# Average pooling of a 3-D volume: the early store goes back into one queue, and TensorE takes over the wait for the stores

## The chip, the core and the metric

The kernel runs on one core of a Trainium2 chip. The metric is the device time of one execution in microseconds; the kernel before has a median of 91.88 us over three executions (91.84 to 92.04). A core has five engines that run their own instruction streams: TensorE (PE), VectorE (DVE), ScalarE (ACT), GpSimd (POOL) and SyncE (SP). They meet at semaphores, which are small counters. Transfers between the chip's memory (HBM) and the core's on-chip memory (SBUF, 128 partitions) are issued by SP or ACT, each into a queue of its own, and are carried out by 16 DMA engines. A transfer adds 1 to its semaphore 16 times, once for each DMA engine, as the parts land.

## The reference

The input is x, 8 x 32 x 32 x 32 x 32 in float32 (33.55 MB). The output is the mean of each 2 x 2 x 2 window over the last three dimensions, 8 x 32 x 16 x 16 x 16 (4.19 MB):

```python
for i in range(out_d):
    for j in range(out_h):
        for k in range(out_w):
            window = x[:, :, 2*i:2*i+2, 2*j:2*j+2, 2*k:2*k+2]
            result[:, :, i, j, k] = np.mean(window, axis=(-3, -2, -1))
```

## The kernel before

Batch and channel together are 256 rows, which are two halves of 128 partitions (t = 0 and 1). A row of the input is 32768 floats, cut into 128 pieces of KF = 256 floats. The list `plan` cuts each half into four units of 32 pieces, 32 KB per partition and 4 MB in all. The last two units are each loaded and pooled in two parts of 16 pieces, so there are ten loads: six of 4 MB and four of 2 MB. The tile `tin` has five buffers, so the sixth, seventh and eighth unit wait until VectorE is done with the first, second and third.

For each part `pool_unit` runs three VectorE operations: pairs of planes are added (L58), then neighbours in a row (L62), and then pairs of lines, scaled by 1/8, into `obuf` (L65). A small instruction that reads VectorE's accumulator into `dummy` follows each. There is one `obuf` per half, 16 KB per partition.

All ten loads are issued by SP (L77), in order. The first was moved ahead of the opening barrier. Four stores (L92) take the output out. ACT issues the first: 2 KB per partition of half 0, as soon as the first unit is pooled. SP issues the others after all its loads: the remaining 14 KB per partition of half 0, then 14 KB of half 1, which waits for all but the last part, and then the last 2 KB of half 1. A queue's transfers are started in the order of their issue, so the large stores stand behind the loads in SP's queue.

The end of the program is written out by hand (L119 to L161). The list `kept` holds the semaphores that the stores update. The block `closing` has SP's waits for all other semaphores, a barrier of the five engines (L102 in the profile; GpSimd gathers and releases it with semaphores 96 and 97), GpSimd's clearing of the semaphores that are not kept (L151, an instruction for each stretch of numbers), and then, on SP, one EventSemaphore for each kept semaphore (L155): it waits until the store has landed and subtracts what was added, so that the semaphore is back at zero. Nothing stands behind these in the program. In the built program the kept semaphores are 102, 103, 104 and 105: 102 belongs to ACT's store and afterwards to the last load, 103 to 105 each to an early load and then to a store.

Of the kernel before, what the change touches and what calls it, by code (L numbers as in the profile page):

```python
# [1 line left out]

# [4 lines left out]

F32 = mybir.dt.float32
KF = 256


@with_exitstack
def pool_rows(
    ctx: ExitStack,
    tc: tile.TileContext,
    x: bass.AP,
    kernel_size: int,
    out: bass.AP,
):
    nc = tc.nc  # L20
    assert kernel_size == 2, "only kernel_size == 2 supported"

    B, C, D, H, W = x.shape
    P = nc.NUM_PARTITIONS
    assert (B * C, D, H, W) == (2 * P, 32, 32, 32)
    add = mybir.AluOpType.add

    xv = x.rearrange("b c d h w -> (b c) (d h w)")  # L30
    ov = out.rearrange("b c d h w -> (b c) (d h w)")

    pool_in = ctx.enter_context(tc.tile_pool(name="pin", bufs=5))
    pool_out = ctx.enter_context(tc.tile_pool(name="pout", bufs=1))
    obuf = [pool_out.tile([P, 16 * KF], F32, name=f"obuf{t}") for t in range(2)]
    dummy = pool_out.tile([P, 1], F32, name="dummy")


    plan = [
        (0, 0, (32,)),
        (0, 32, (32,)),
        (0, 64, (32,)),
        (0, 96, (32,)),
        (1, 0, (32,)),
        (1, 32, (32,)),
        (1, 64, (16, 16)),
        (1, 96, (16, 16)),  # L50
    ]

    def pool_unit(buf, t, k0, kb):

        od = kb // 8
        a = buf.rearrange("p (o dd e) -> p o dd e", o=od, dd=2)
        b = buf[:, :od * 1024]
        nc.vector.tensor_add(  # L58
            out=b.rearrange("p (o e) -> p o e", o=od), in0=a[:, :, 0], in1=a[:, :, 1])
        bv = b.rearrange("p (e ww) -> p e ww", ww=2)  # L60
        c = buf[:, od * 1024:od * 1536]
        nc.vector.tensor_add(out=c, in0=bv[:, :, 0], in1=bv[:, :, 1])  # L62
        cv = c.rearrange("p (j hh k) -> p j hh k", hh=2, k=16)
        o0 = k0 * KF // 8
        nc.vector.tensor_tensor_reduce(  # L65
            out=obuf[t][:, o0:o0 + od * 256].rearrange("p (j k) -> p j k", k=16),
            in0=cv[:, :, 0], in1=cv[:, :, 1],
            scale=0.125, scalar=0.0, op0=add, op1=add, accum_out=dummy[:, :],
        )

    for t, k0, parts in plan:
        tin = pool_in.tile([P, 32 * KF], F32, tag="tin", name="tin")
        views = []
        o = 0
        for kb in parts:
            v = tin[:, o * KF:(o + kb) * KF]
            nc.sync.dma_start(  # L77
                out=v, in_=xv[t * P:(t + 1) * P, (k0 + o) * KF:(k0 + o + kb) * KF])
            views.append((v, k0 + o, kb))
            o += kb  # L80
        for v, k, kb in views:
            pool_unit(v, t, k, kb)

    for queue, t, k0, kb in [
        (nc.scalar, 0, 0, 2),
        (nc.sync, 0, 2, 14),
        (nc.sync, 1, 0, 14),
        (nc.sync, 1, 14, 2),  # L90
    ]:
        queue.dma_start(  # L92
            out=ov[t * P:(t + 1) * P, k0 * KF:(k0 + kb) * KF],
            in_=obuf[t][:, k0 * KF:(k0 + kb) * KF],
        )


def kernel(tc: tile.TileContext, x: bass.AP, kernel_size: int, out: bass.AP):
    nc = tc.nc
    pool_rows(tc, x, kernel_size, out)  # L100
    tc.close()
    tc.compile()  # L102
    blocks = nc.main_func.blocks

    opening, program = blocks[0].instructions, blocks[tc.starting_block_idx].instructions
    load = next(i for i in program if isinstance(i, mybir.InstDMACopy))
    assert load.engine == nc.sync.engine
    barrier = next(  # L110
        n for n, i in enumerate(opening)
        if i.engine == load.engine and isinstance(i, mybir.InstDrain))
    program.remove(load)
    opening.insert(barrier, load)

    closing = blocks[-1].instructions  # L119
    stores = [  # L120
        i for i in program
        if isinstance(i, mybir.InstDMACopy) and "out_" in i.outs[0].memref]
    kept = [u.id for i in stores for u in i.sync_info.on_update]
    kept = [n for j, n in enumerate(kept) if n not in kept[j + 1:]]
    final = next(
        i for i in closing
        if i.engine == nc.sync.engine and isinstance(i, mybir.InstDrain))
    waits = {w.id: w for w in final.sync_info.on_wait}
    closing[closing.index(final)] = mybir.InstDrain(
        name=final.name, engine=final.engine, ins=[], outs=[], is_reset_sema=False,  # L130
        sync_info=mybir.SyncInfo(
            on_wait=[w for n, w in waits.items() if n not in kept], on_update=[]))


    reset = next(
        n for n, i in enumerate(closing)
        if isinstance(i, mybir.InstDrain) and i.is_reset_sema)
    first, stop = closing[reset].reset_range_start, closing[reset].reset_range_stop
    assert isinstance(closing[reset + 1], mybir.InstISA)
    while len(closing) > reset:  # L140
        closing.pop()
    n = first
    while n < stop:
        m = n
        while m < stop and m not in kept:
            m += 1
        if m > n:
            closing.append(mybir.InstDrain(
                name=nc.get_next_instruction_name(), engine=nc.gpsimd.engine, ins=[], outs=[],
                is_reset_sema=True, reset_range_start=n, reset_range_stop=m))  # L150
            nc.gpsimd.sem_clear(range(n, m))  # L151
        n = m + 1
    for n in kept:
        w = waits[n]
        closing.append(mybir.InstEventSemaphore(  # L155
            name=nc.get_next_instruction_name(), engine=nc.sync.engine, ins=[], outs=[],
            sync_info=mybir.SyncInfo(
                on_wait=[w],
                on_update=[mybir.SyncUpdate(
                    sync_type="semaphore", id=n, ant_name=w.ant_name,  # L160
                    update_mode="sem-sub-imm", update_value=w.wait_value)])))  # L161


# [1 line left out]
_INS = ['x', 'kernel_size']  # L165
_OUTS = [((8, 32, 16, 16, 16), 'float32')]

_NUMBERS = {'kernel_size': 2}


# [26 lines left out]
```

## Time and profile before

| what | value |
|---|---|
| median of three executions | 91.88 us (91.84 to 92.04) |
| profiled execution, its own time | 91.84 us |
| its span, first to last instruction | 86.9 us |
| the time outside the span | 4.94 us |
| VectorE busy | 64.0 us |
| DMA, mean rate over the span | 422 GB/s |
| read, written | 33.55 MB, 4.19 MB |

The span ends with GpSimd's clearing of semaphores. The four EventSemaphores on SP that wait for the stores carry no source line and are not among the instructions of the profile, nor is what the runtime does after the program. The trace does record each update of each semaphore with its time, after the span too; times of updates below are counted from the start of the span, as all others are. "Landing" is the last of a transfer's 16 updates. A row of the instruction list such as "SPq" or "PEldq" is an instruction of that engine's sequencer, not of the engine's arithmetic.

### The profile page before, as it was taken

The numbers are of one execution on the slowest core, as the hardware profiler recorded it, in microseconds if no ns is written. First come the engines' busy times: TensorE is split into PE (matmuls) and PEld (weight loads), VectorE is DVE, ScalarE is ACT, GpSimd is POOL, SyncE is SP. The second block draws the span as 40 slices with busy tenths as digits, with TensorE's granted clock in tenths as the row PEclk, the third lists the DMA queues.
The fourth block names the chain that finished last, engine by engine and source line by source line (L and its number), as shares of the span: only waits on it lengthen the run. The fifth ranks groups of instructions, "written<-read, shape, count | busy, mean of one in ns | idle before, by whom it ended". The sixth has DMA issues, their size and how long they took to land.

```text
span 86.9 us, 90 instructions
## 1 busy us (share of the span) xinstructions
DVE 64.0 (74%) x40; POOL 0.2 (0%) x4
## 2 busy tenths in 40 slices
DVE  0000049992999729994799929994899999999994
POOL 0000000000000000000000000000000000000000
DMA  8989998899969969998899988998999999999999
GB/s 241 392 347 468 483 483 362 377 468 483 478 291 493 513 290 469 483 483 362 377 468 483 483 347 377 483 483 362 415 430 430 415 452 400 468 377 368 422 429 442
DMA packets 1798, 36.66 MB, mean 422 GB/s; under 512 B 192, under 2 KB 192, under 8 KB 320
## 3 DMA queue, kind: packets, MB, share of 16 engines
q1 hardware_dynamic: 1654, 36.39, 98.7%
q10 hardware_dynamic: 144, 0.26, 0.8%
HBM read 33.55 MB, written 4.19 MB: 434 GB/s over the span
## 4 chain that ended last, share of the span: by engine, by line
DMA 61%; DVE 37%; issue 0%; DVEq 0%
DMA tin<-in_x_dram 61%; DVE tin L58 20%; DVE tin L62 11%; DVE obuf L65 6%; DVE dummy L65 0%; DVEq L102 0%
## 5 line engine op out<-in xcount | busy, mean ns | idle before, releaser
L58 DVE TENSOR_TENSOR tin<-tin 128x4096 f32<-128x4096 f32 (+1 forms) x10 | 35.7, 3570 | 21.1 <-DMA tin<-in_x_dram 21.1
L62 DVE TENSOR_TENSOR tin<-tin 128x2048 f32<-128x2048 f32 (+1 forms) x10 | 18.6, 1865 | 0.3
L65 DVE CUSTOM_DVE_ANT_1 obuf<-tin 128x1024 f32<-128x1024 f32 (+1 forms) x10 | 10.1, 1011 | 0.3
L65 DVE DVE_READ_ACCUMULATOR2_ANT dummy<- 128x1 f32 x10 | 0.8, 83 | 0.0
L178 POOL MEMSET const-bfloat16-1.0<- 128x1 bf16 x1 | 0.1, 101 | 0.0
L178 POOL MEMSET const-uint8-127<- 128x1 uint8 x1 | 0.1, 101 | 0.0
L178 POOL MEMSET const-float32-0.0<- 128x1 f32 x1 | 0.1, 98 | 0.2 <-issue 0.2
L178 POOL MEMSET const-float32-1.0<- 128x1 f32 x1 | 0.1, 98 | 0.0
## 6 DMA issues: line engine op xcount, KB each, us to landing
tin<-in_x_dram SPq DMA_DIRECT2D x6, 4096.0 KB, 35.5
tin<-in_x_dram SPq DMA_DIRECT2D x4, 2048.0 KB, 38.5
out_dram<-obuf SPq DMA_DIRECT2D x2, 1792.0 KB, 22.0
out_dram<-obuf ACTq DMA_DIRECT2D x1, 256.0 KB, 14.1
out_dram<-obuf SPq DMA_DIRECT2D x1, 256.0 KB, 4.6
```

The source lines that it names most:

```text
L58: nc.vector.tensor_add(out=b.rearrange("p (o e) -> p o e", o=od), in0=a[:, :, 0], in1=a[:, :, 1])
L62: nc.vector.tensor_add(out=c, in0=bv[:, :, 0], in1=bv[:, :, 1])
L65: nc.vector.tensor_tensor_reduce(out=obuf[t][:, o0:o0 + od * 256].rearrange("p (j k) -> p j k", k=16), in0=cv[:, :, 0], in1=cv[:, :, 1], s ...
L178: nc = _bacc.Bacc("TRN2", target_bir_lowering=False, num_devices=1)
```

## The change

The early store on ACT's queue is dropped, and the store of half 0 on SP's queue is the whole half, 16 KB per partition in place of 14. The two stores of half 1 are as they were. The EventSemaphores at the end are put on TensorE in place of SP. In the built program there are now three of them, for semaphores 102, 103 and 104; the semaphores of the loads are numbered anew, and SP's waits before the closing barrier gain one instruction. ACT is left with nothing but the barriers.

```diff
-    for queue, t, k0, kb in [
-        (nc.scalar, 0, 0, 2),
-        (nc.sync, 0, 2, 14),
-        (nc.sync, 1, 0, 14),
-        (nc.sync, 1, 14, 2),
-    ]:
-        queue.dma_start(
+    for t, k0, kb in [(0, 0, 16), (1, 0, 14), (1, 14, 2)]:
+        nc.sync.dma_start(
             out=ov[t * P:(t + 1) * P, k0 * KF:(k0 + kb) * KF],
             in_=obuf[t][:, k0 * KF:(k0 + kb) * KF],
         )
...
     for n in kept:
         w = waits[n]
         closing.append(mybir.InstEventSemaphore(
-            name=nc.get_next_instruction_name(), engine=nc.sync.engine, ins=[], outs=[],
+            name=nc.get_next_instruction_name(), engine=nc.tensor.engine, ins=[], outs=[],
             sync_info=mybir.SyncInfo(
                 on_wait=[w],
```

## The prediction

> **What bounds the kernel now.** I read the page first, for the DMA row, the queues and the issues; then the order of time, for when loads land; then the windows near the end; then the list of the closing barrier's instructions; and last the record of semaphore updates behind the span.
>
> ```profile
> span 86.9 us, 90 instructions
> DVE 64.0 (74%) x40; POOL 0.2 (0%) x4
> ...
> DMA  8989998899969969998899988998999999999999
> ...
> q1 hardware_dynamic: 1654, 36.39, 98.7%
> q10 hardware_dynamic: 144, 0.26, 0.8%
> ...
> out_dram<-obuf SPq DMA_DIRECT2D x2, 1792.0 KB, 22.0
> out_dram<-obuf ACTq DMA_DIRECT2D x1, 256.0 KB, 14.1
> out_dram<-obuf SPq DMA_DIRECT2D x1, 256.0 KB, 4.6
> ```
>
> The packets of both queues together fill 99.5% of the 16 DMA engines' span, and the DMA row is full to its end. VectorE is idle for a quarter of the span. The last store is issued at 85.83 us and lands 4.6 us later: it waits behind the two large stores. So the DMA engines bound the kernel from the first load to the last store, though the chain on the page ends on VectorE. What counts is the sum of the packets, and then what follows the last landing.
>
> ```profile
> 20.14 0.38 ACTq L92 DMA_DIRECT2D out_dram<-obuf  x1
> 21.79 4.42 DVE L58 TENSOR_TENSOR tin<-tin 128x4096 f32<-128x4096 f32 x1 [1.68 <-DMA tin<-in_x_dram]
> 32.08 4.43 DVE L58 TENSOR_TENSOR tin<-tin 128x4096 f32<-128x4096 f32 x1 [2.27 <-DMA tin<-in_x_dram]
> 41.81 4.42 DVE L58 TENSOR_TENSOR tin<-tin 128x4096 f32<-128x4096 f32 x1 [1.72 <-DMA tin<-in_x_dram]
> 51.52 4.43 DVE L58 TENSOR_TENSOR tin<-tin 128x4096 f32<-128x4096 f32 x1 [1.69 <-DMA tin<-in_x_dram]
> ```
>
> A first addition starts when its 4 MB have landed. Undisturbed, loads land 9.71 us apart (41.81 to 51.52). The load beside ACT's store took 10.29, and 2.27 us of idle time on VectorE show it.
>
> The close. The last update of the last store's semaphore comes at 90.446 us; SP takes the semaphore back at 90.480. After that semaphore 2 is updated in rounds of nine. Four updates had come already, at 86.855, 86.889, 87.441 and 87.486; the other five come at 90.603, 90.646, 90.685, 90.719 and 90.766. Then five blocks of semaphores are zeroed, and a second round of nine follows, from 91.597 to 91.955. I read a round as the five engines passing a token up (four hops, the fifth engine turns it) and down again. The fifth is SP, since it alone was still waiting. GpSimd is the third, since it comes late (87.441), after its two clears. I take the first for TensorE: the block of numbers up to 53, zeroed last, goes at 7 to 10 ns a number where SP's takes about 2, and TensorE is the slow sequencer in the closing barrier:
>
> ```profile
> L102 SPq EVENT_SEMAPHORE  x1: 17/17/17, 86.6 to 86.6; - x1
> L102 ACTq EVENT_SEMAPHORE  x1: 17/17/17, 86.6 to 86.6; - x1
> L102 DVEq EVENT_SEMAPHORE  x1: 21/21/21, 86.6 to 86.6; - x1
> L102 PEldq EVENT_SEMAPHORE  x1: 51/51/51, 86.6 to 86.6; - x1
> ```
>
> The reader is to see 51 ns against 17. So today the wait sits on the engine that turns the token: four hops are done in the shadow of the stores, and the way down takes 0.163 us (90.603 to 90.766).
>
> **The change, part by part.** The sum is made against the profiled execution, 91.84 us, which stands 0.04 below the median.
>
> *ACT's store goes.* By the trace's packets it is 8 of 2 KB at 84 ns on each DMA engine and one of 9 ns for the semaphore: 8 x 84 + 9 = 0.681 us. By landings, the loads that ended at 32.053 and 41.788 took together 20.03 us, where two undisturbed ones take 2 x 9.712: 0.60. So 0.60 to 0.68 us are given back, and every load from the third on lands that much earlier.
>
> *Half 0's store grows from 14 to 16 KB a row.* A 14336-byte packet of a store takes 535 ns and a 16384-byte packet of a load 611, the same 26.8 bytes per ns, so I take 611: 8 x (611 - 535) = 0.608 us. The store waits in SP's queue behind the loads in any case and meets no free time there. Both parts: between 0.608 - 0.681 = -0.07 and 0.608 - 0.60 = +0.01; I take -0.03.
>
> A rule speaks against this half of the change. The Trainium skill, page Perfetto Trace Analysis, section DMA Optimizations, advises giving loads one issuing engine and stores another, for a more dynamic spread. If the early store on its own queue thereby rode free, dropping it would give nothing back, the 0.61 would remain, and the sum would be 0.61 + 0.36 = 0.97 over before, 92.85 us; the row of 10.29 us against 9.71 says that it did not ride free.
>
> *VectorE and SP.* VectorE's last 24.6 us run without a pause from the load that lands at 61.21, so they move with it by 0.6 us: the store of half 1 is issued at about 81.0 in place of 81.63, the last one at 85.2. SP's queue is busy with half 0's store until about 85.6, so neither leaves the DMA engines without work: nothing. Should that cover go, a late last store would cost its issue to landing alone. One more EventSemaphore on SP ahead of the barrier (28 ns, as its two neighbours) and GpSimd's clear of one number more (45 to 51 ns a clear) end before 87.5, some 3 us before the stores: nothing, and at most 0.1 without that cover. SP issues one large store of the same count; ACT issues none (0.38 us of its own sequencer, for which nobody waited).
>
> *TensorE waits in SP's place.* Three terms. First, from the landing to the semaphore taken back: SP needs 34 ns (90.446 to 90.480). In the closing barrier both wait for the same update at 86.541; SP takes its count back at 86.575, TensorE at 86.632, that is 34 and 91 ns: +0.057. Second, from there to the engine's step of the round: SP 0.123 (90.480 to 90.603), TensorE 0.223 (86.632 to 86.855, and 0.224 from its last zeroed number at 91.373 to the second round): +0.100. Third, the round: TensorE starts it, so no hop can be done ahead, and it takes as long as the second round, 0.358 (91.597 to 91.955), or as the last one ahead of the span, 0.370, in place of 0.163: +0.195 to +0.207. Queued behind the waiting instruction on TensorE is only that step, and all four other engines wait for it; SP, which waited so far, is then one of them. Sum +0.352 to +0.364; I take +0.355. Bounds: no less than 0.034, the difference of the two instructions, if TensorE is not at the head and its longer step overlaps the wait; no more than 0.40, with 0.262, the longest pause seen on that engine in the close (90.766 to 91.028), as its step. I stay near the upper end, since 0.223 and 0.358 are the same work in the same trace.
>
> Sum: 91.84 - 0.03 + 0.355 = 92.165 for an execution like the profiled one; plus 0.04 for the median, 92.20 us, 0.35% over before.
>
> **The rivals.**
>
> *The slow stretch goes* (not slower). Near the end of the loads the transfers slow down:
>
> ```profile
> 77.00:78.00 1.00, 1.00 (x3) 0.00 (x0) 1.00 1.14 442
> 78.00:79.00 1.00, 1.00 (x1) 0.00 (x0) 1.00 0.94 279
> 79.00:80.00 1.00, 0.97 (x2) 0.00 (x0) 1.00 0.96 393
> ```
>
> The last column is GB/s: 279 in one microsecond. The last load landed at 81.231, 5.333 us after the one before, where the three before it took 4.89 to 4.90; its 16 updates spread over 0.55 us in place of 0.36. The mean of the 16 is late by 0.28 and the last by 0.43. If the disorder that ACT's packets bring is its cause, and it goes with them, the last landing gains up to 0.43 and the sum is -0.07 + 0.355 - 0.43 = -0.15: 91.7 to 91.9. It decides from 0.15 us of gain, where what is left is within the measurement. For it: no other load is stretched so. Against it: ACT's last packets are 44 us earlier, and the five loads between run at full rate.
>
> *The close is not where the time is.* If the round's head is another engine, or the time is taken before the round, only 0.034 to 0.157 of the close remains, with the -0.03: 91.9 to 92.0. For it: no row names the engine of an update of semaphore 2. Against it: the time outside the span, 4.94 us, reaches to 91.84 when it is counted from the span's start, past the second round's start at 91.597.
>
> *The early store rode free after all*, so that the loads speed up by less than 0.608: slower by up to 0.608 + 0.355, 92.84. Against it stands the row of 10.29.
>
> **How the numbers follow.** A measurement of this kernel can tell about 0.2%, 0.18 us, from no change. My forecast has a chance of 0.70, its own range 92.05 to 92.35: slower nearly always (0.68). The stretch gone 0.13: within the bound mostly, a few faster (0.07 and 0.06). The close elsewhere 0.10: within the bound (0.09). The store that rode free 0.07: slower. Together slower 0.76, the same 0.18, faster 0.06. The range goes from 91.85, in the middle of the first rival, to 92.5, half way to the last, which is room for another stretch of 0.3 us.
>
> **What would show it.** In the changed kernel the loads of 4 MB land 9.71 us apart throughout; the sixth unit's first addition starts at about 60.6 in place of 61.23; the span shrinks by about 0.6 us to 86.3 while the time grows, so that the time outside it is about 5.9 us in place of 4.94. Stores' packets of 16384 bytes take 611 ns. The last landing stays at 90.4. Semaphore 2 is not updated between the opening and the last store's landing; then all nine updates come together, the first some 0.31 us after the landing and the ninth some 0.36 after that. Four updates at about 87 us, as before, would prove the order wrong; a last landing off 90.4 by over 0.2 would put the error into the transfers.

## The result and the profile after

The changed kernel takes 92.33 us (median of six executions, 92.21 to 92.54); six executions of the kernel before, beside it, have a median of 92.06 (91.84 to 92.11). The two medians lie 0.27 us apart. The ratio, taken over all the executions, is 1.0037, with a 95% interval of 1.0020 to 1.0053: the change costs about 0.34 us (0.18 to 0.49).

The page of the changed kernel, the lines that answer to those shown of before:

```profile
span 86.4 us, 90 instructions
...
DMA  8969997999979999699979999699999999998999
...
q1 hardware_dynamic: 1638, 36.43, 99.4%
...
out_dram<-obuf SPq DMA_DIRECT2D x1, 2048.0 KB, 36.4
out_dram<-obuf SPq DMA_DIRECT2D x1, 1792.0 KB, 9.0
out_dram<-obuf SPq DMA_DIRECT2D x1, 256.0 KB, 5.3
```

One queue is left and its packets fill the 16 DMA engines as the two did (99.4% against 99.5%). The span is 0.5 us shorter, though the execution is longer: the profiled one took 92.31 us, 5.91 outside its span in place of 4.94. The order of time shows the loads, now undisturbed; the columns are start, duration, engine, line, operation, and the idle time before it:

```profile
21.81 4.43 DVE L58 TENSOR_TENSOR tin<-tin 128x4096 f32<-128x4096 f32 x1 [1.69 <-DMA tin<-in_x_dram]
31.52 4.42 DVE L58 TENSOR_TENSOR tin<-tin 128x4096 f32<-128x4096 f32 x1 [1.69 <-DMA tin<-in_x_dram]
41.24 4.42 DVE L58 TENSOR_TENSOR tin<-tin 128x4096 f32<-128x4096 f32 x1 [1.70 <-DMA tin<-in_x_dram]
...
49.29 36.33 SPq L86 DMA_DIRECT2D out_dram<-obuf  x3
...
60.69 4.43 DVE L58 TENSOR_TENSOR tin<-tin 128x4096 f32<-128x4096 f32 x1 [1.70 <-DMA tin<-in_x_dram]
```

The third unit starts at 31.52 in place of 32.08 and the sixth at 60.69 in place of 61.23. What the loads gain there the larger store of half 0 takes back: its landing comes 4.90 us after the last load's (means over the 16 updates), where the 14 KB store took 4.30. The last store's semaphore is full at 90.566 us, against 90.446.

The rest is the close, the time from the last landing to the last update of semaphore 2, which no row of the profile shows. The record of semaphore updates does; in us from the last landing:

| | before | changed |
|---|---|---|
| the semaphore is taken back | 0.034 | 0.091 |
| first round: updates that came before the landing | 4 | 0 |
| first round: first update after the landing | 0.157 | 0.358 |
| first round: last update | 0.320 | 0.716 |
| block up to number 53 zeroed, last of it | 0.927 | 1.280 |
| second round: first, last update | 1.151, 1.509 | 1.504, 1.861 |

Between the two profiled executions lie 92.31 - 91.84 = 0.47 us: 0.352 of it is the close (1.861 - 1.509) and 0.12 the later last landing. The profiled time ends 0.115 us (before) and 0.117 us (changed) short of the last update of semaphore 2, both counted from the start of the span; over all thirteen profiled executions of this study it is 0.115 to 0.127. So what lengthens the close lengthens the measured time by as much.

### The profile page after: what moved, and what is told of

It reads as the page before. It is cut to its first block, busy times and chain, and to the rows that moved or that the text cites. A ratio compares the mean times of both kernels' runs of the same rounds, so it can differ in the third digit from the quotient of the medians.

```text
span 86.4 us, 90 instructions
## 1 busy us (share of the span) xinstructions
DVE 64.0 (74%) x40; POOL 0.2 (0%) x4
## 3 DMA queue, kind: packets, MB, share of 16 engines
q1 hardware_dynamic: 1638, 36.43, 99.4%
## 4 chain that ended last, share of the span: by engine, by line
DMA 61%; DVE 37%; issue 0%; DVEq 0%
DMA tin<-in_x_dram 61%; DVE tin L58 21%; DVE tin L62 11%; DVE obuf L65 6%; DVE dummy L65 0%; DVEq L96 0%
```

## The experiments

The question was whether the wait's engine is the whole cost, and by which mechanism, and whether the moved store costs or gains anything. The close is read from the trace to some ns; the ratios tell about 0.15% either way. In the expectations, A is that the wait's place in the round and TensorE's slow sequencer are the whole cost, B that the moved store has a part in it, and C that TensorE's sequencer alone is dear.

**The wait alone.** The kernel before, with the last loop's engine changed:

```diff
-            name=nc.get_next_instruction_name(), engine=nc.sync.engine, ins=[], outs=[],
+            name=nc.get_next_instruction_name(), engine=nc.tensor.engine, ins=[], outs=[],
```

> The four stores stay as before, ACT's early one too; only the wait moves to TensorE. Theory A (the wait's place in the round and TensorE's slow sequencer are the whole cost, the stores cost nothing): +0.35 us, ratio 1.0039; from the last landing to the last update of semaphore 2 it takes 1.86 us as in the changed kernel, against 1.51 before; the first four updates of the round come after the landing. Theory B (0.12 us of the cost is the later last landing of the changed kernel, so the merged store's): about +0.23 us, 1.0025, with the last landing at 90.45.

Ratio 1.0032 (1.0015 to 1.0049). The close is 1.864 us, and all nine updates of the first round come after the landing, as in the changed kernel. ACT's store is there again and delays its load as before:

```profile
20.23 0.37 ACTq L92 DMA_DIRECT2D out_dram<-obuf  x1
21.87 4.43 DVE L58 TENSOR_TENSOR tin<-tin 128x4096 f32<-128x4096 f32 x1 [1.67 <-DMA tin<-in_x_dram]
32.14 4.42 DVE L58 TENSOR_TENSOR tin<-tin 128x4096 f32<-128x4096 f32 x1 [2.26 <-DMA tin<-in_x_dram]
```

The idle time of 2.26 us is that of before (2.27), while the cost is that of the whole change. Its last landing was at 90.551, as late as that of the changed kernel though its stores are those of before. This run alone does not decide against theory B: its interval holds B's 1.0025 too, and the last landing of one execution says little, since those of the merged kernels below range from 90.39 to 90.84. The next two runs decide it.

**The merge alone.** The changed kernel with `engine=nc.sync.engine` in the last loop. It ran twice.

> The early store is merged into half 0's store, SP still waits. Theory A: -0.03 us, between -0.07 and +0.01, ratio 0.9997; the close is 1.51 us from the last landing as before; the last landing at 90.3 to 90.5. Theory B: +0.12 us, 1.0013, the last landing at 90.57 as in the changed kernel.

> The merge alone with SP waiting, again. By packets 0.03 to 0.07 us under before, ratio 0.9993 to 0.9997; if the merge gains more than its packets, 0.9985 or under as the first time.

Ratios 0.9989 (0.9972 to 1.0006) and 0.9994 (0.9980 to 1.0008): no difference that can be told, with the estimate of -0.03 us inside both. Theory B asks for 1.0013, above both intervals, and falls. The close is 1.509 and 1.511 us, that of before. The last landings were 90.790 and 90.561, above the expected 90.3 to 90.5: the last load landed 5.58 and 5.37 us after the one before it (means over the 16 updates), where an undisturbed one takes 4.89. That is the slow stretch of the last section.

**The change once more, beside the merge.** The changed kernel as it is, in the comparison of the merge's second run.

> The changed kernel once more, beside the next two on the same chip, to see whether its cost is that of the wait alone plus that of the merge alone (1.0032 and 0.9989 so far, 1.0021 together) or more (1.0037 so far). By the closes and the packets: +0.35 - 0.03 = +0.32 us, 1.0035, and 0.35 us over the merge with SP waiting. If the two halves act on one another: over 1.0045.

Ratio 1.0039 (1.0024 to 1.0055), and 1.0039 - 0.9994 = 0.0045, 0.41 us, over the merge in the same comparison; the closes differ by 0.353 (1.864 against 1.511). The two halves do not act on one another by anything that these intervals show.

**Other engines in TensorE's place.** The changed kernel with one word changed: `nc.scalar`, `nc.vector` or `nc.gpsimd` for `nc.tensor`. If only TensorE's slow sequencer were dear, ACT and VectorE would cost nothing.

> The changed kernel with ACT in TensorE's place. Theory A with the place in the round: ACT takes the semaphore back after 0.045 us, steps as SP does after 0.12, and the round from the second place to the end takes 0.32 in place of 0.16: the close is 1.51 + 0.17 = 1.68 us, the time +0.14 with the -0.03 of the stores. Theory C (TensorE's sequencer alone is dear, the place in the round is not): the close is 1.52, the time as before.

> The changed kernel with VectorE in TensorE's place. Theory A: VectorE is the fourth of the round; back after 0.057 us, a step of 0.12, and 0.24 in place of 0.16 for the rest of the round: the close is 1.51 + 0.10 = 1.61 us, the time +0.07. Theory C: the close is 1.53, the time as before.

> The changed kernel with GpSimd in TensorE's place, behind its clears. It should be the third of the round: of the first round two updates come before the landing and seven after it. From its step the rest of the round takes 0.29 us in place of 0.16. Its own step took 0.53 us after its last clear in the kernel before (86.906 to 87.441), and 0.12 on SP: the close is 1.51 + 0.13 = 1.64 us if that long step belongs to the clears, and 1.51 + 0.13 + 0.41 = 2.05 if it is GpSimd's own. A round that did not count (theory C) would show 1.51 to 1.92 by the same two.

From the semaphore record, in us; "ahead" is the number of the first round's updates that came before the last landing, "rest" the time from the waiting engine's step to the ninth update:

| waits | ahead | taken back | its step after that | rest | close | ratio (95%) |
|---|---|---|---|---|---|---|
| SP (before) | 4 | 0.034 | 0.123 | 0.163 | 1.509 | 1 |
| VectorE | 3 | 0.058 | 0.188 | 0.241 | 1.676 | 0.9993 (0.9977 to 1.0009) |
| GpSimd | 2 | 0.049 | 0.566 | 0.284 | 2.089 | 1.0054 (1.0037 to 1.0071) |
| ACT | 1 | 0.045 | 0.133 | 0.325 | 1.690 | 1.0011 (0.9995 to 1.0027) |
| TensorE (changed) | 0 | 0.091 | 0.267 | 0.358 | 1.861 | 1.0037 (1.0020 to 1.0053) |

The number ahead names each engine's place: TensorE first, ACT second, GpSimd third, VectorE fourth, SP fifth. The rest of the round grows with each place ahead of SP's, as expected to within 0.01 us. So the place in the round has its price, whatever the engine, and theory C falls on its closes. The engine's own step is the second term, and it is not small: GpSimd, two places nearer to the end than TensorE, is the dearest of all, because its step takes 0.566. Of its two expected closes (1.64 and 2.05) the second held: the long step belongs to the engine and not to the clears. VectorE's step of 0.188, where 0.12 was assumed, makes its close 1.676 in place of 1.61; its ratio does not show it: the interval ends at 1.0009, and the close with the packets' -0.03 asks for 1.0015. That stays unexplained. Its profiled execution lacks the slow stretch of the others near 77 us, but lost 0.49 us in earlier loads (last section), and its last landing, 90.393, is close to that of before.

**The last wait on SP, the two others on TensorE.**

```diff
-            name=nc.get_next_instruction_name(), engine=nc.tensor.engine, ins=[], outs=[],
+            name=nc.get_next_instruction_name(),
+            engine=(nc.sync if n == kept[-1] else nc.tensor).engine, ins=[], outs=[],
```

It ran twice:

> The changed kernel, but SP waits for the last store alone and TensorE for the two before. By the round, TensorE steps 0.36 us after the second last landing, which is 0.5 before the last, so the token reaches SP just as the last store lands: the close is 1.51 us as with SP alone, the time as the merge alone, 0.997 to 1.000. If waiting instructions on TensorE cost by themselves, the close is 1.6 to 1.9.

> SP waits for the last store, TensorE for the two before, again. Its close was 1.477 us in place of 1.509: 0.03 us under the merge alone if that holds in the time, ratio 0.9989 to 0.9995.

The first four updates come 0.236 to 0.120 us before the last landing (0.243 to 0.127 the second time), behind the store before it, and the close is 1.477 and 1.479 us. Waiting on TensorE costs nothing so long as it ends before the token is due at SP. That close is 0.03 us shorter than with SP alone: TensorE starts to zero its block 0.216 us after its last step of the round, in place of 0.262. In the time nothing of it can be seen: ratios 0.9989 (0.9975 to 1.0003) and 1.0001 (0.9985 to 1.0016). No version with the whole output beats the kernel before by more than the measurement can tell.

**The price of the early store.** SP waits; the first 2 KB per partition of half 0's output are left out:

```diff
-    for t, k0, kb in [(0, 0, 16), (1, 0, 14), (1, 14, 2)]:
+    for t, k0, kb in [(0, 2, 14), (1, 0, 14), (1, 14, 2)]:
```

> As the merge alone with SP waiting, but the first 2 KB per partition of half 0's output are not stored at all. This prices the 256 KB. If the early store on ACT's queue cost its packets: 0.60 to 0.68 us under before, ratio 0.993; and 0.61 under the merge alone. If it rode free beside the loads: as before, and 0.61 under the merge alone, which would then be 0.6 over before.

Ratio 0.9921 (0.9903 to 0.9938), 0.73 us under before; 0.60 to 0.68 were expected and the interval holds them. It was 0.9989 for the merge alone, in another comparison, so the 256 KB cost 0.6 to 0.7 us in either place. They did not ride free.

**The whole store of half 0 on ACT's queue.** SP waits:

```diff
-        nc.sync.dma_start(
+        (nc.scalar if t == 0 else nc.sync).dma_start(
```

> SP waits at the end, and the whole store of half 0 (2 MB) goes on ACT's queue, issued at about 49.3 us beside the loads. If a store on a second queue takes the loads' bandwidth byte for byte: the loads behind it land 4.9 us later, the last at about 85.6, VectorE ends at about 90, the last store is issued after that and lands at 92.5 to 93: 2.0 to 2.6 us over before, ratio 1.022 to 1.028. If it rides free in part: the last landing comes at 90.4 or sooner, ratio 1.00 or under.

Ratio 1.0171 (1.0150 to 1.0193), 1.57 us over before: of the expected sign, but less than the expected 2.0 to 2.6. The throughput row of its page and its last two stores, then its order of time:

```profile
GB/s 229 459 430 401 344 444 444 459 459 459 459 430 387 358 444 444 459 459 459 459 430 373 344 315 430 487 401 409 401 430 452 437 401 430 452 444 394 79 439 386
...
out_dram<-obuf SPq DMA_DIRECT2D x1, 1792.0 KB, 5.8
out_dram<-obuf SPq DMA_DIRECT2D x1, 256.0 KB, 2.2
```

```profile
58.95 0.08 DVE L65 DVE_READ_ACCUMULATOR2_ANT dummy<- 128x1 f32 x1
65.69 4.42 DVE L58 TENSOR_TENSOR tin<-tin 128x4096 f32<-128x4096 f32 x1 [6.66 <-DMA tin<-in_x_dram]
...
86.08 4.54 SPq L86 DMA_DIRECT2D out_dram<-obuf  x2
...
90.17 0.08 DVE L65 DVE_READ_ACCUMULATOR2_ANT dummy<- 128x1 f32 x1
```

VectorE is idle for 6.66 us before the sixth unit, which starts at 65.69 in place of 60.69; the store landed at 67.48. From the next load on, the loads land 5.6 us later than in the changed kernel (means over the 16 updates); for the last it is 5.3, since that one was stretched there and is not here. The store's packets are worth 4.9 us. The other 0.7 us were lost while the store ran: 32 of the loads' packets of 32768 bytes took 1.38 to 1.88 us between 50.3 and 56.7 us, in place of 1.21. Whether the second queue or a slow stretch as in the last section made them slow no run shows.

VectorE then ends at 90.25. The large store of half 1, issued at 86.08, finds its queue empty: the last load's last packet had ended at 85.38 and the store's first started at 86.92, so the DMA engines had no packet for 1.5 us. That is the 79 GB/s in the third slice from the end. The last store follows directly behind it and lands at 92.517, at the lower end of what was expected. The profiled execution, 93.91 us, was the longest of the four, which go down to 93.46. The spans of the other three are 0.2 to 0.3 us shorter, so most of their gain lies ahead of VectorE's end; what it is no trace shows.

This is the case of the rule that the prediction weighed, the Trainium skill, page Perfetto Trace Analysis, section DMA Optimizations: loads on one issuing engine and stores on another, which the page says may make sense. In this kernel, whose DMA engines are full, the separate queue let the large store overtake the loads, and the kernel was 1.7% slower.

## Why the prediction was right

**The transfers.** They were costed at -0.03 us (-0.07 to +0.01), and two measurements of the merge alone agree with that (0.9989 and 0.9994), though neither can tell it from nothing (both have 1 in the interval). The loads of the changed kernel land 9.70 to 9.72 us apart. Half 0's store took 4.896 us in landings, and 8 x 611 + 9 ns is 4.897: a store's 16384-byte packet costs what a load's does. The sixth unit started at 60.69, not 60.6: its load gained 0.62 us in the mean of its 16 updates, but 0.55 in the last, which is the one waited for. No cost of VectorE's head start or of SP's extra instruction can be seen, as forecast. The last landing, forecast to stay at 90.4, came at 90.566, and at 90.793 in the second profile of the same kernel. The prediction had said that a landing off by over 0.2 would put the error into the transfers. Between these two profiles it is the last load that differs: it took 5.23 and 5.55 us.

**The close.** It was the sum's large term, +0.355 us, and it measured +0.352, but its parts were not all of that size:

| part | predicted | measured |
|---|---|---|
| the semaphore taken back, TensorE less SP | +0.057 | +0.057 |
| the engine's step | +0.100 | +0.144 |
| the round from that step to its end | +0.195 to +0.207 | +0.195 |
| from there to the second round | 0 | -0.044 |

The last row is the difference of 1.151 - 0.320 = 0.831 us (before) and 1.504 - 0.716 = 0.788 (changed). TensorE's step took 0.267 us where 0.223 was taken over from the closing barrier; its zeroing then began 0.215 us after its last step in place of 0.262. The step even passed the 0.262 of the prediction's upper bound. The prediction had neither of these 45 ns, and that they cancel was luck. They do not belong together: in the two runs with the last wait on SP, where TensorE had two waits in place of three, it stepped after 0.223 us and yet began to zero after 0.216 and 0.215. What makes up either no run shows.

**The place of the engines.** That TensorE is the first and SP the fifth was argued from a slow block of numbers and a barrier's row of 51 ns; the experiments with other engines show it. The Trainium skill, page Runtime: NRT & Kernel Launch, section The ~15µs preamble/postamble breakdown, gives a serpentine across the five engines, for the barrier ahead of the program, 8 hops of 44 ns and about 355 ns in all. The whole round behind the program measured 0.358 us here; its single hops took 23 to 98 ns.

**The rivals.** The slow stretch did not go. The windows of the changed kernel, with GB/s in the last column:

```profile
77.00:78.00 1.00, 1.00 (x1) 0.00 (x0) 1.00 1.25 459
78.00:79.00 1.00, 1.00 (x1) 0.00 (x0) 1.00 0.93 262
79.00:80.00 1.00, 0.97 (x2) 0.00 (x0) 1.00 0.88 377
```

There are 262 GB/s from 78 to 79 us where the kernel before had 279, with no ACT store in the program at all, so that store was not its cause. The close was in the time: the wait alone, with the stores of before, cost 1.0032. And the early store had not ridden free.

The median forecast, 92.20 us, was built on a median of 91.88 over three executions; six gave 92.06. So the 92.33 came out at the top of its own range, 92.05 to 92.35. The step up, +0.325 us by the sum, is what held: 0.34 by the ratio.

## What to carry to other kernels

These are shown on this kernel alone. At the end of a program, put the last wait on an engine that the closing round reaches late and whose own step is short; SP here is both. Let no other engine hold what the round must pass on its way; waits that end a few tenths of a microsecond earlier may stand anywhere. When the DMA engines are full, moving a small store between queues gains nothing that can be told, and a large store that overtakes loads starves the engine that feeds the last stores. A page whose span shrinks while the time grows says that the cost lies behind the last instruction that the profile lists; look for it in the semaphore updates.

## What was not expected

The slow stretch did not go with ACT's store. Of the thirteen profiled executions of this study ten show packets stretched between about 76.5 and 79.5 us from the first instruction, with the loads 0.6 us earlier or not, with ACT's store or without, with TensorE, ACT, GpSimd or SP waiting. These are windows of the merge alone:

```profile
76.00:77.00 1.00, 0.96 (x4) 0.00 (x0) 1.00 1.04 393
77.00:78.00 1.00, 1.00 (x1) 0.00 (x0) 1.00 1.00 279
78.00:79.00 1.00, 1.00 (x1) 0.00 (x0) 1.00 0.95 279
```

The last load then lands 5.18 to 5.64 us after the one before it (means over the 16 updates), in place of 4.89. That is 0.3 to 0.75 us, as much as the change itself. The kernel without the early part shows it faintly (4.99). VectorE's and the one with half 0 on ACT's queue don't show it at that time (4.90 and 4.89).

These three lost time earlier instead. With VectorE waiting, the fourth to sixth load landed 9.78, 9.97 and 9.88 us apart in place of 9.71, 0.49 us in all. Without the early part, the third to sixth were 9.76 to 9.85 apart, 0.37 us in all. With half 0 on ACT's queue, 0.7 us went between 50 and 57 us, as told above. In the last of these another load ran at the time of the stretch, undisturbed, and the last load, some 5 us later, was undisturbed too. So neither the last load's addresses nor the time alone is the cause; what it is stays open. Of the 0.12 us between the two last landings of the profiles it accounts for half (5.23 against 5.18); nearly all the rest is how far the last of the 16 updates trails their mean.

GpSimd takes 0.566 us from the semaphore taken back to its step of the round, four times SP's 0.128 in the same form of program, and VectorE 0.188. TensorE, slow as its 51 ns instruction looked, is the dearest engine to end on but for that one, more than half of it by its place (0.195 of 0.352 us).
